# A hybrid decoder layer in float32: two more raw chunks in the up projection's ring, and four plain units at the head of the first down pair

## The chip, the cores and the metric

The kernel runs on one NeuronCore of a Trainium2 chip. The metric is the device time of one launch, in microseconds. Before the change the median of three runs was 1467.55 us (1465.33 to 1468.01). The engines are called TensorE (PE; its weight loads are PEld), VectorE (DVE), ScalarE (ACT), GpSimd (POOL) and SyncE (SP). SP and POOL issue the DMAs.

## The reference, cut to what matters

One layer of a decoder with 256 tokens and a width of 2048, in float32. The change touches the second half, the convolutional feed-forward part, and its weights `w_up` (2048 x 11264) and `w_down` (5632 x 2048):

```python
def conv_ffn(h, w_up, conv_w, conv_b, w_down):
    S = h.shape[1]
    a, b = jnp.split(h @ w_up, 2, axis=-1)
    ap = jnp.pad(a, ((0, 0), (CONV_WIDTH - 1, 0), (0, 0)))
    c = conv_b
    for j in range(CONV_WIDTH):
        c = c + conv_w[j] * ap[:, j:j + S]
    return (jax.nn.gelu(c, approximate=True) * b) @ w_down

def reference(x, ...):
    h = rms_norm(x, norm_mix_pre[l])
    y = hybrid_mixer(h, ...)              # latent attention, windowed attention, gates, output projection
    x = x + rms_norm(y, norm_mix_post[l])
    h = rms_norm(x, norm_ffn_pre[l])
    y = conv_ffn(h, ffn_w_up[l], ffn_conv_w[l], ffn_conv_b[l], ffn_w_down[l])
    return x + rms_norm(y, norm_ffn_post[l])
```

## The kernel before

**Arithmetic.** Every large product runs in a float32 format that TensorE takes at full rate, with each operand split into a high part and a low remainder. A product of two operands is three matmuls (high by high, high by low, low by high), which `mm3` issues. Weights come from HBM as a raw float32 chunk of 128 x 1024 (512 KB). `convert` (L135) then makes two tiles of it: ACT casts the raw chunk to `whi` (L144), and DVE subtracts that from the raw chunk to get `wlo` (L145). So each chunk needs one DMA, one ACT pass, one DVE pass, and then its matmuls.

**The rings.** Raw chunks lie in a ring of `RAW = 3` tiles, converted pairs in a ring of `RING = 4` pairs. Two more tiles, the `flex` tiles, serve either as two more raw chunks or as one more converted pair; `flex[0]` says which, and `in_turn` (L111) decides for each new chunk. `more_raw` is a list of makers of raw tiles through which `raw_row` (L151), the loader of single rows of weights, turns when it is not empty; `wchunk` (L117), the loader of the general chunks, doesn't look at it. A raw tile is free again once ACT and DVE have read it, a converted pair once PE has.

**Order of the work.** The program is traced in one order, with a clock of steps: each chunk of a product ends with `tick()`, and `at(t, f)` puts a piece of other work at step t. A planner then orders each engine's instructions by this trace order, by when their inputs should be there and by when a buffer is free; it can issue work earlier than it was traced where its buffer is free (the parked copies of the residual, traced in c = 2, run before the up projection). Each engine, and each DMA queue's issuer, works through its list in order: an instruction that waits holds up all behind it.

**The up projection.** `ffn_up0` makes the first 512 columns of both halves, then `ffn_up(c, ...)` (L1269) runs for c = 1 to 5 and, after the first part of the down projection, for c = 6 to 10. Each makes 512 columns of the activation half and 512 of the gate half with one call of `gemm_cols` (L1250) for each: eight chunks, and for each chunk eight matmuls of 512 columns (L1257, weight high by activations high and low) and eight of 256 (L1261, weight low by activations high). Tiles `ua` and `ub` are the two accumulators. `evac` brings them out (L1278 and L1279), and `conv_cols` (L1148) does the convolution, the GELU and the split of the result in four pieces, at the steps 1, 3, 5 and 7 of the chunks that follow.

**The down projection.** After c = 5, 24 of the 44 blocks of 128 inner columns are there. `pair_gemm` (L253) takes them in 12 units of two blocks, for 1024 output columns at a time; two such pairs, `d0` and `d1`, make the 2048 columns. A *plain* unit (letter p) converts two rows of weights and needs 8 products, 24 matmuls of 512 columns. A *seven* unit (letter s) uses a scheme of seven products, 21 matmuls; it needs sums of the tokens and sums of the weights, and 3.5 chunks of raw data: two of stored sums, one row and a half row of weights. `PAIR_ORDER` gives the order of the letters; the seven units take the first units in number, the plain ones the rest. At the start of the pairs the `flex` tiles turn to raw chunks, and eight steps later `deep_raws` (L1317) turns them back and puts seven raw tiles into `more_raw`: the ring and four tiles that held the evacuated accumulators.

**The sums.** `park_sums` (L221) makes the weight sums of a seven unit ahead of time: POOL loads two chunks into one tile of 128 x 2048 with the tag `gp` (L229), DVE makes four subtractions in it (L233), POOL stores the two halves to DRAM (L238, L243). Four units are done early; the others run during c = 1 to c = 4, one every 7 or 8 steps. `g_sums(u)` (L1242) makes the token sums of unit u, with `token_sums` (L347 to L353) and a split (L386, L387): six DVE instructions and one of ACT. Its results lie in tiles of two units each: units 0 and 1 in the tile of the first half of the tokens' residual (tag `x2_0`), 2 and 3 in that of the second half (`x2_1`), 4 and 5 in `gp`. Those two tiles are free because `park` (L1228) has stored the residual to DRAM; it is loaded again near the end.

After c = 10 the rest of the inner columns goes through another pair and two plain products.

Of the kernel before, what the change touches and what calls it, by code (L numbers as in the profile page):

```python
# [11 lines left out]
F32 = mybir.dt.float32  # L12
# [7 lines left out]
P = 128  # L20
D = 2048
# [21 lines left out]
def trunk_layer(ctx, tc, x, x_cols_in, conv_cols_in, g_mix_post, g_ffn_post, w_in, w_q, w_kv,  # L43
# [16 lines left out]
    def sb(pl, shape, name, dt=F32, tag=None, bufs=None):  # L60
        return pl.tile(shape, dt, name=name, tag=tag or name, **({"bufs": bufs} if bufs else {}))
# [46 lines left out]
    def ring_tile(kind, name, dt, extra):  # L108
        pl_tag = dict(name=name, tag="flex", bufs=2) if extra else dict(name=name, tag=kind, bufs=RAW if kind == "raw" else RING)
        return ring.tile([P, 1024], dt, **pl_tag)  # L110

    def in_turn(kind):

        turn[kind] += 1
        return flex[0] == kind and turn[kind] % (RAW + 2 if kind == "raw" else RING + 1) >= (RAW if kind == "raw" else RING)

    def wchunk(src, shape, own=None, rawp=None, rbufs=1, parts=None):  # L117
        i = cnt[0]
        cnt[0] += 1
        n = int(np.prod(shape))  # L120
        raw = rawp.tile([P, 1024], F32, name=f"raw{i}", tag="xraw", bufs=rbufs) if rawp else \
            ring_tile("raw", f"raw{i}", F32, in_turn("raw"))
        dst = raw[:, :n]
        if len(shape) == 2:
            dst = dst.rearrange("p (a b) -> p a b", a=shape[0])
        elif len(shape) == 3:
            dst = dst.rearrange("p (a b c) -> p a b c", a=shape[0], b=shape[1])
        if len(shape) == 3:
            for k in range(shape[0]):
                nc.sync.dma_start(dst[:, k], src[:, k])  # L130
        else:
            nc.sync.dma_start(dst, src)
        return convert(raw, n, own=own, parts=parts)
# [11 lines left out]
            vec.tensor_tensor(lo[:, a:b], raw[:, a:b], hi[:, a:b].bitcast(F32), op=ALU.subtract)  # L145
        return hi, lo

    more_raw = []
    raw_of = lambda name: ring_tile("raw", name, F32, False)

    def raw_row(src, n=1024):  # L151
        i = cnt[0]
        cnt[0] += 1
        if more_raw:
            make = more_raw.pop(0)
            more_raw.append(make)
            raw = make(f"raw{i}")
        else:
            raw = ring_tile("raw", f"raw{i}", F32, in_turn("raw"))
        nc.sync.dma_start(raw[:, :n], src)  # L160
        return raw

    steps = defaultdict(list)
    now = [0]

    def at(t, *fs):
        steps[max(t, now[0])].extend(fs)
# [53 lines left out]
    def park_sums(name, w, k, c0, pl, tag, t0, bufs=None):  # L221

        td = [dram.tile([P, 1024], F32, name=f"{name}{i}") for i in range(2)]
        st = []

        def load():
            st.append(sb(pl, [P, D], f"{name}s", tag=tag, bufs=bufs))
            for i in range(2):
                pool.dma_start(st[0][:, i * 1024:(i + 1) * 1024], w[(k + i) * P:(k + i + 1) * P, c0:c0 + 1024])  # L229

        def less(o, x, y):
            o, x, y = (st[0][:, i * 512:(i + 1) * 512] for i in (o, x, y))
            tc.keep_in_program_order(vec.tensor_tensor(o, x, y, op=ALU.subtract))  # L233

        def even():
            less(0, 1, 0)
            less(1, 3, 1)
            pool.dma_start(td[0], st[0][:, 0:1024])  # L238

        def odd():  # L240
            less(3, 3, 0)
            less(2, 2, 3)
            pool.dma_start(td[1], st[0][:, 1024:2048])  # L243

        at(t0 - 5, load)
        at(t0, even)
        at(t0 + 1, odd)
        return td

    def park_a(i, pl, tag, t0, **kw):  # L250
        return park_sums(f"ta{i}_", w_down, 2 * (i % NA), 1024 * (i // NA), pl, tag, t0, **kw)

    def pair_gemm(name, w, k0, c0, order, act_of, s_of, kind, d, place=None, sums=None, parked=None):  # L253

# [478 lines left out]
    acc, _ = gemm(XH, XL, w_in, 0, KT, 0, 512)  # L733
# [4 lines left out]
    acc, _ = gemm(XH, XL, w_in, 0, KT, C_KV, KVR + ROPE)  # L738
# [71 lines left out]
    parked_a = [park_a(i, pg, "gr", now[0] + 5 + 5 * i, bufs=2) for i in range(EARLY)]  # L810
# [158 lines left out]
    for j in range(4):  # L969
        acc, _ = gemm(XH, XL, w_in, 0, KT, C_GA + 512 * j, 512)  # L970
# [9 lines left out]
    es3, p3 = open_pool("p3")  # L980
# [49 lines left out]
    for j in range(4):  # L1030
# [4 lines left out]
        acc, _ = gemm(AH, AL, wo_a, 0, KT, 512 * j, 512, ps=(pss, "s") if j == 3 else None)  # L1035
# [190 lines left out]
    gtiles, s_pool, s_of = [], [], {}  # L1226

    def park(t, j):  # L1228
        pool.dma_start(x2_d[t, :, j * 512:(j + 1) * 512], x2[t][j])
# [4 lines left out]
        c = slice(j * 512, (j + 1) * 512)  # L1234
        nc.sync.dma_start(x2_all[t][:, c], x2_d[t, :, c])

    s_tiles = []

    def sums_tile(name, i):
        return sb(*((p3,) if i < 2 else (p6,)), [P, D], f"{name}_{i}", F32R, tag=(f"x2_{i}" if i < 2 else "gp"))  # L1240

    def g_sums(u):  # L1242

        if u % 2 == 0:
            s_tiles.append(sums_tile("s", u // 2))
        hi, lo = (s_tiles[u // 2][:, (u % 2) * 1024 + i * 512:(u % 2) * 1024 + (i + 1) * 512] for i in range(2))
        a, m = (sb(s_pool[0], [P, 512], f"s{n}{u}", tag="hx", bufs=2) for n in "am")
        s_of[u] = token_sums(gtiles[u].bitcast(F32), a, m, hi, lo)
# [40 lines left out]
            at(now[0] + 1 + 2 * i, lambda i=i: conv_cols(4 * c + i, sa[0][i], sa[1][i], slot0 + i))  # L1289

    es7 = ffn_up0()
    for i in range(2 * NA - EARLY):
        parked_a.append(park_a(i + EARLY, p6, "gp", now[0] + 8 + 15 * i // 2))
    for c in range(1, 6):
        if c == 2:
            for i in range(8):
                at(now[0] + i, lambda i=i: park(i // 4, i % 4))
        if c == 4:
            for u in range(4):
                at(now[0] + 3 + 3 * u, lambda u=u: g_sums(u))  # L1300
        if c == 5:
            for u in range(4, NA):
                at(now[0] + 3 + 5 * (u - 4), lambda u=u: g_sums(u))
        ffn_up(c, 4 * c)

    def down(k0, nk, c0, n, split=None, ps=None):
# [16 lines left out]
    for p in range(2):  # L1323
        d = [dsum[t][2 * p + j] for t in range(NT) for j in range(2)]
        c = pair_gemm(f"d{p}", w_down, 0, 1024 * p, PAIR_ORDER[p], lambda k, t: (GH(k)[:, t * P:(t + 1) * P], GL(k)[:, t * P:(t + 1) * P]),
                      lambda u: s_of[u], p, d, parked=parked_a[NA * p:NA * (p + 1)])
        for n_, (o, x_) in enumerate(zip(d, c)):
            at(now[0] + n_, lambda o=o, x_=x_: vec.tensor_tensor(o, o, x_, op=ALU.add))
    more_raw.clear()
# [11 lines left out]

    parked_b = [park_sums(f"tb{i}_", w_down, 24 + 2 * i, 0, p6, "gp", now[0] + 6 + 8 * i) for i in range(NB_)]
    for c in range(6, 11):
        if c == 9:
            for u in range(NB_):
                at(now[0] + 2 + 4 * u, lambda u=u: b_sums(u))
        ffn_up(c, 4 * (c - 6))
# [174 lines left out]
```

## Time and profile before

| | |
|---|---|
| median of three runs | 1467.55 us |
| runs, lowest and highest | 1465.33 and 1468.01 us |
| the profiled execution, its own time | 1472.41 us |
| its span, first to last instruction | 1470.6 us |
| granted TensorE clock over the span | 0.998 |
| up projection c = 1 to 5, with the end of `ffn_up0` | 776.1 to 1006.3 us |
| the two down pairs | 1006.3 to 1133.3 us |
| up projection c = 6 to 10 | 1133.3 to 1357.7 us |

The page counts an engine as busy from the start of an instruction to its modelled end. Matmuls are pipelined, and PE is shown as busy for almost the whole span; lost time is better seen in how long a fixed piece of work takes, for instance one call of `gemm_cols`, which is always the same 128 matmuls. The idle time of ACT and DVE costs nothing as long as PE finds its weights converted.

### The profile page before, as it was taken

How to read it: one execution, taken by the hardware profiler on the slowest of the kernel's cores; microseconds unless marked ns; L12 is line 12 of the kernel's file. 1: busy time of each engine (PE TensorE's matmuls, PEld its weight loads, DVE VectorE, ACT ScalarE, POOL GpSimd, SP SyncE). 2: the span in 40 equal slices, each digit the busy share in tenths (PEclk: the TensorE clock that was granted, in tenths of full speed). 3: DMA queues.
4: the chain of work that ended last, by engine and by line, in shares of the span. 5: the costliest groups of instructions: out<-in, count | busy, mean ns of one | idle time of the engine just before them, and what ended most of it. 6: DMA issues, size and time to landing. Idle time of an engine off the chain costs nothing.

```text
span 1470.6 us, 21276 instructions
## 1 busy us (share of the span) xinstructions
PE 1453.6 (99%) x7543; PEld 1239.7 (84%) x7543; DVE 1119.9 (76%) x1959; ACT 850.3 (58%) x1403; POOL 98.6 (7%) x176
## 2 busy tenths in 40 slices
PE   9999999999999999999999999999999999999997
PEld 7888888888888888888888888787888888888886
DVE  7788896766667666768799877677777778887776
ACT  7588874544565554446666554565655555566653
POOL 0012110010000011100000001000000000000000
PEclk9999999999999999999999999999999999999999
DMA  8755386697665559765767778777887888767973
GB/s 294 218 173 164 96 271 195 213 338 243 187 160 156 172 168 335 258 185 176 223 215 222 259 264 286 244 221 264 276 276 264 274 270 263 247 207 252 334 240 133
DMA packets 163302, 339.53 MB, mean 231 GB/s; under 512 B 20171, under 2 KB 31340, under 8 KB 163196
## 3 DMA queue, kind: packets, MB, share of 16 engines
q1 hardware_dynamic: 145888, 277.25, 59.4%
q0 software_dynamic: 17216, 60.88, 12.2%
q8 instruction: 59, 0.97, 0.3%
q14 instruction: 47, 0.39, 0.1%
q10 hardware_dynamic: 92, 0.05, 0.0%
HBM read 310.82 MB, written 27.31 MB: 230 GB/s over the span
## 4 chain that ended last, share of the span: by engine, by line
PE 75%; DVE 10%; DMA 9%; ACT 3%; issue 2%; DVEq 0%; ACTq 0%; SPq 0%
PE accg L184 12%; PE accg L186 12%; PE accg L185 12%; DMA raw<-in_ffn_w_up_dram 8%; PE ua L1257 4%; DVE wlo L145 4%; PE ub L1257 3%; PE ua L1261 2%; PE cd L185 2%; PE cd L186 2%; PE cd L184 2%; ACT whi L144 2%; PE ub L1261 2%; DVE ta_s L233 1%; PE mpo L948 1%
## 5 line engine op out<-in xcount | busy, mean ns | idle before, releaser
L145 DVE TENSOR_TENSOR wlo<-raw,whi 128x1024 fp32r<-128x1024 f32 (+2 forms) x526 | 624.5, 1195 | 243.0 <-ACT whi L144 238.0
L144 ACT CAST whi<-raw 128x1024 fp32r<-128x1024 f32 (+2 forms) x526 | 537.0, 1028 | 431.0 <-PE accg L186 157.3
L184 PE MATMUL accg<-whi,ahl 128*128 128x512 f32 (+1 forms) x416 | 162.8, 391 | 0.0
L186 PE MATMUL accg<-whi,ahl 128*128 128x512 f32 (+1 forms) x416 | 160.6, 386 | 0.0
L185 PE MATMUL accg<-wlo,ahl 128*128 128x512 f32 (+1 forms) x416 | 159.8, 384 | 0.0
L1257 PE MATMUL ub<-ahl,whi 128*128 128x512 f32 x640 | 154.6, 391 | 0.0
L1257 PE MATMUL ua<-ahl,whi 128*128 128x512 f32 x640 | 154.6, 391 | 0.0
L184 PE MATMUL accg<-whi,bhl 128*128 128x512 f32 x378 | 148.2, 392 | 0.0
L186 PE MATMUL accg<-whi,bhl 128*128 128x512 f32 x378 | 147.4, 390 | 0.0
L185 PE MATMUL accg<-wlo,bhl 128*128 128x512 f32 x378 | 147.3, 390 | 0.0
L1257 PEld LDWEIGHTS ua<-ahl,whi 128*128 128x128 f32 x640 | 117.6, 188 | 22.7
L1257 PEld LDWEIGHTS ub<-ahl,whi 128*128 128x128 f32 x640 | 117.5, 188 | 22.6
L186 PEld LDWEIGHTS accg<-whi,ahl 128*128 128x128 f32 x416 | 78.1, 188 | 15.5
L1261 PEld LDWEIGHTS ub<-ahl,wlo 128*128 128x128 f32 x640 | 82.5, 191 | 8.1 <-DVE wlo L145 4.8
L185 PEld LDWEIGHTS accg<-wlo,ahl 128*128 128x128 f32 x416 | 78.2, 188 | 13.1
L184 PEld LDWEIGHTS accg<-whi,ahl 128*128 128x128 f32 x416 | 78.2, 188 | 13.0
L1261 PE MATMUL ub<-ahl,wlo 128*128 128x256 f32 x640 | 84.5, 283 | 4.0 <-DVE wlo L145 4.0
L1261 PEld LDWEIGHTS ua<-ahl,wlo 128*128 128x128 f32 x640 | 82.4, 191 | 5.1 <-DVE wlo L145 1.9
L1261 PE MATMUL ua<-ahl,wlo 128*128 128x256 f32 x640 | 84.4, 283 | 1.5 <-DVE wlo L145 1.5
L186 PEld LDWEIGHTS accg<-whi,bhl 128*128 128x128 f32 x378 | 71.0, 188 | 14.8
L185 PEld LDWEIGHTS accg<-wlo,bhl 128*128 128x128 f32 x378 | 71.0, 188 | 14.4
L184 PEld LDWEIGHTS accg<-whi,bhl 128*128 128x128 f32 x378 | 71.0, 188 | 14.4
(573 smaller groups left out, 2336.8 us busy)
## 6 DMA issues: line engine op xcount, KB each, us to landing
raw<-in_ffn_w_up_dram SPq DMA_DIRECT2D x176, 512.0 KB, 4.7
raw<-in_w_in_dram SPq DMA_DIRECT2D x105, 512.0 KB, 4.6
raw<-in_ffn_w_down_dram SPq DMA_DIRECT2D x70, 512.0 KB, 5.2
raw<-in_w_o_swa_dram SPq DMA_DIRECT2D x32, 512.0 KB, 4.9
raw<-in_w_o_mla_dram SPq DMA_DIRECT2D x32, 512.0 KB, 5.0
raw<-in_w_out_dram SPq DMA_DIRECT2D x26, 512.0 KB, 4.2
ta_s<-in_ffn_w_down_dram POOLq DMA_DIRECT2D x24, 512.0 KB, 6.2
ta<-ta_s POOLq DMA_DIRECT2D x24, 512.0 KB, 5.2
```

The costliest lines, as they stand in the source:

```text
L144: act.copy(hi[:, a:b], raw[:, a:b])
L145: vec.tensor_tensor(lo[:, a:b], raw[:, a:b], hi[:, a:b].bitcast(F32), op=ALU.subtract)
L184: pe.matmul(o, ah, bh, start=start, stop=False)
L185: pe.matmul(o, ah, bl, start=False, stop=False)
L186: pe.matmul(o, al, bh, start=False, stop=stop)
L233: tc.keep_in_program_order(vec.tensor_tensor(o, x, y, op=ALU.subtract))
L948: pe.matmul(o, w(t), p_[:, c], start=n == 0, stop=n == 5)
L1257: pe.matmul(acc[i], hi[:, c], hn[p][:, j * 512:(j + 1) * 512], start=p + j == 0, stop=stop)
L1261: pe.matmul(acc[i][:, 0:256], lo[:, c], hn[p][:, j * 512:j * 512 + 256], start=False, stop=False)
```

## The change

There are two parts.

First, the choice of a raw tile moves into a function `new_raw`, which takes its tiles from `more_raw` when that list is not empty, and `wchunk` uses it as well as `raw_row`. A new function `x_raws` takes a tile with the tag `x2_1`, the one that held the second half of the residual, and fills `more_raw` so that the raw ring's three tiles alternate with the two halves of that tile: five raw chunks in place of three. It runs at step 8 of c = 2, and the list is emptied at step 6 of c = 5; it runs again at step 1 of c = 6 and is emptied at step 5 of c = 9. Since `x2_1` is taken in that time, the token sums of units 2 and 3 move: units 0 and 1 are traced in c = 4, and in c = 5 come units 4, 5, 2 and 3, at the steps 0, 4, 8 and 11.

Second, the order of the first down pair has four plain units at its head and five of seven products in all, in place of two and six. `NA` becomes a list with the number of seven units of each pair, so that eleven pairs of weight sums are stored in place of twelve.

```diff
+    more_raw = []
+    raw_of = lambda name: ring_tile("raw", name, F32, False)
+
+    def new_raw(name):
+        if not more_raw:
+            return ring_tile("raw", name, F32, in_turn("raw"))
+        more_raw.append(more_raw.pop(0))
+        return more_raw[-1](name)
+
     def wchunk(src, shape, own=None, rawp=None, rbufs=1, parts=None):
...
-            ring_tile("raw", f"raw{i}", F32, in_turn("raw"))
+            new_raw(f"raw{i}")
...
     def raw_row(src, n=1024):
         i = cnt[0]
         cnt[0] += 1
-        if more_raw:
-            make = more_raw.pop(0)
-            more_raw.append(make)
-            raw = make(f"raw{i}")
-        else:
-            raw = ring_tile("raw", f"raw{i}", F32, in_turn("raw"))
+        raw = new_raw(f"raw{i}")
...
     def park_a(i, pl, tag, t0, **kw):
-        return park_sums(f"ta{i}_", w_down, 2 * (i % NA), 1024 * (i // NA), pl, tag, t0, **kw)
+        u, p = (i, 0) if i < NA[0] else (i - NA[0], 1)
+        return park_sums(f"ta{i}_", w_down, 2 * u, 1024 * p, pl, tag, t0, **kw)
...
+    def x_raws():
+        t = sb(p3, [P, D], f"xraw{now[0]}", tag="x2_1")
+        more_raw[:] = [raw_of, lambda name: t[:, 0:1024], raw_of, lambda name: t[:, 1024:2048], raw_of]
...
-    for i in range(2 * NA - EARLY):
+    for i in range(sum(NA) - EARLY):
         parked_a.append(park_a(i + EARLY, p6, "gp", now[0] + 8 + 15 * i // 2))
     for c in range(1, 6):
         if c == 2:
             for i in range(8):
                 at(now[0] + i, lambda i=i: park(i // 4, i % 4))
+            at(now[0] + 8, x_raws)
         if c == 4:
-            for u in range(4):
+            for u in range(2):
                 at(now[0] + 3 + 3 * u, lambda u=u: g_sums(u))
         if c == 5:
-            for u in range(4, NA):
-                at(now[0] + 3 + 5 * (u - 4), lambda u=u: g_sums(u))
+            at(now[0] + 6, more_raw.clear)
+            for u, t in ((4, 0), (5, 4), (2, 8), (3, 11)):
+                at(now[0] + t, lambda u=u: g_sums(u))
         ffn_up(c, 4 * c)
...
-                      lambda u: s_of[u], p, d, parked=parked_a[NA * p:NA * (p + 1)])
+                      lambda u: s_of[u], p, d, parked=parked_a[NA[0] * p:])
...
     for c in range(6, 11):
+        if c == 6:
+            at(now[0] + 1, x_raws)
         if c == 9:
+            at(now[0] + 5, more_raw.clear)
             for u in range(NB_):
                 at(now[0] + 2 + 4 * u, lambda u=u: b_sums(u))
         ffn_up(c, 4 * (c - 6))
...
-PAIR_ORDER = ("ppspspsspssp", "ppspspsspssp")
+PAIR_ORDER = ("ppppspsspssp", "ppspspsspssp")
 EARLY = 4
-NA = PAIR_ORDER[0].count("s")
+NA = [o.count("s") for o in PAIR_ORDER]
```

More of the change, by code (lines that the diff above doesn't have):

```diff
@@ L146, in convert @@
         return hi, lo
-    more_raw = []
-    raw_of = lambda name: ring_tile("raw", name, F32, False)
     def raw_row(src, n=1024):
@@ L1235, in unpark @@
         nc.sync.dma_start(x2_all[t][:, c], x2_d[t, :, c])
-    s_tiles = []
+    s_tiles = {}
     def sums_tile(name, i):
         return sb(*((p3,) if i < 2 else (p6,)), [P, D], f"{name}_{i}", F32R, tag=(f"x2_{i}" if i < 2 else "gp"))
+    def x_raws():
+        t = sb(p3, [P, D], f"xraw{now[0]}", tag="x2_1")
+        more_raw[:] = [raw_of, lambda name: t[:, 0:1024], raw_of, lambda name: t[:, 1024:2048], raw_of]
     def g_sums(u):
         if u % 2 == 0:
-            s_tiles.append(sums_tile("s", u // 2))
+            s_tiles[u // 2] = sums_tile("s", u // 2)
         hi, lo = (s_tiles[u // 2][:, (u % 2) * 1024 + i * 512:(u % 2) * 1024 + (i + 1) * 512] for i in range(2))
```

## The prediction

> **What bounds the kernel now.** I read the page first (engines, chain), then the busy time by stretch over the feed-forward part, then the chain of waits and the waits inside the stretches that stood out.
>
> ```profile
> span 1470.6 us, 21276 instructions
> ...
> PE 1453.6 (99%) x7543; PEld 1239.7 (84%) x7543; DVE 1119.9 (76%) x1959; ACT 850.3 (58%) x1403; POOL 98.6 (7%) x176
> ```
>
> TensorE is the bound, so time can only go where it waits, or through fewer matmuls. I cut the feed-forward part at the first matmul of each call of `gemm_cols` and of the down pairs (rows: stretch, its length, busy time and instructions of PE, PEld, DVE, ACT and POOL, granted clock, DMA share, GB/s):
>
> ```profile
> 867.20:889.40 22.20, 22.20 (x129) 19.66 (x128) 17.42 (x31) 10.31 (x17) 2.13 (x4) 1.00 0.74 238
> 889.40:984.10 94.70, 90.32 (x514) 79.03 (x513) 71.40 (x119) 50.33 (x82) 6.40 (x12) 1.00 0.78 257
> 984.10:1006.30 22.20, 22.20 (x129) 19.65 (x128) 17.03 (x27) 13.11 (x22) 0.00 (x0) 1.00 0.74 225
> 1006.30:1034.00 27.70, 25.56 (x104) 19.94 (x103) 18.50 (x27) 15.58 (x24) 0.00 (x0) 0.94 0.76 266
> 1034.00:1133.30 99.30, 99.30 (x440) 82.23 (x439) 73.64 (x74) 58.94 (x62) 1.06 (x2) 1.00 0.84 279
> ...
> 1222.40:1268.70 46.30, 45.24 (x258) 39.61 (x257) 38.05 (x67) 25.42 (x42) 4.26 (x8) 1.00 0.81 263
> 1268.70:1357.70 89.00, 89.00 (x513) 78.67 (x513) 69.27 (x115) 54.04 (x88) 1.07 (x2) 1.00 0.73 231
> ```
>
> An undisturbed call takes 89.00 / 4 = 22.25 us (last row), that is 2.78 us for each of its 8 chunks of 512 KB. Three places lose time. 889.4 to 984.1 holds four calls (second half of c = 3 to the first half of c = 5): 94.7 - 89.0 = **5.7 us lost**. 1222.4 to 1268.7 holds two (c = 8): 46.3 - 44.5 = **1.8 us**. The two down pairs have 2 x (6 x 24 + 6 x 21) = 540 matmuls; 438 of them fill the 99.3 us from 1034.0 (the row counts two more, cut by its edges), 0.227 us each; the other 102 should take 23.1 us and took 27.7: **4.6 us** at the head of the first pair. Together 12.1 us; everywhere else here PE runs without a break, and that is the ceiling of any gain.
>
> What the up projection waits for, in the chain of waits (start, duration, what) and in the waits of 889 to 984 (total, times, longest):
>
> ```profile
> 938.04 1.06 ACT whi L144
> 939.12 1.24 DVE wlo L145
> 940.37 9.95 DMA raw<-in_ffn_w_up_dram
> 950.41 1.05 ACT whi L144
> ```
> ```profile
> ACT whi L144 <- DMA raw<-in_ffn_w_up_dram: 28.4, 14, 6.2
> ```
> ```profile
> SPq L132 <- DVE wlo L145: 28.6, 15, 3.2
> ```
> ```profile
> raw<-in_ffn_w_up_dram SPq DMA_DIRECT2D x65, 512.0 KB, 4.8
> ta_s<-in_ffn_w_down_dram POOLq DMA_DIRECT2D x14, 512.0 KB, 6.6
> ```
>
> The first rows are one turn of the raw ring: DVE finishes a chunk, only then does SP issue the load that takes its slot, and ACT starts when that lands. A slot is held for load + cast + subtraction: 4.8 (median of the third fence) + 1.05 + 1.24 = 7.1 us, with the 9.95 us load 12.2 us. Three slots come round every 3 x 2.78 = 8.3 us. The median just fits, any load over 6.0 us doesn't, and the lead in converted weights is eaten until PE stops. Loads get that long while POOL loads a parked pair beside them:
>
> ```profile
> 939.80 1.06 POOL L229 DMA_DIRECT2D ta_s<-in_ffn_w_down_dram  x2 [5.96 <-DMA ta<-ta_s]
> ```
>
> **The change, part by part.**
>
> *Five raw slots instead of three, c = 2 to c = 5 and c = 6 to c = 9.* Five slots come round every 13.9 us, more than the longest slot time above (12.2 us). So the waits of both up stretches should go. Not all of it: at 5.7 + 1.8 us I keep 1.3, because DVE also stands before the parked rows, and because the engines are fuller in the stretch that loses first:
>
> ```profile
> 889.40:912.70 23.30, 22.67 (x129) 19.79 (x129) 17.90 (x31) 11.91 (x21) 2.58 (x5) 1.00 0.90 315
> ...
> 961.20:984.10 22.90, 22.59 (x131) 19.76 (x129) 18.69 (x33) 13.81 (x23) 0.00 (x0) 1.00 0.68 198
> ```
>
> The bounds are 0 saved (that 0.90 is a ceiling) and 7.5; without the waits the stretch needs 257 x 94.7 / 89.0 = 273 GB/s, below the 315 that were moved, so I stand near the upper end: **-6.2 us**.
>
> *Where the two slots come from.* The second residual tile has to be parked before. Its stores were issued at 739.4 and took 5.7 us in the median, 100 us before the tile is wanted (c = 2, step 8, two calls before 889), so SP never stands at its first load:
>
> ```profile
> 739.40 2.53 POOL L1229 DMA_DIRECT2D x_d<-x  x4 [3.28 <-DVE x L1068]
> ```
> ```profile
> x_d<-x POOLq DMA_DIRECT2D x8, 256.0 KB, 5.7
> ```
>
> In the second half the tile is free when units 2 and 3 of the second pair are done, the eighth of its twelve units, some 20 us before c = 6. Cost 0; without that cover SP, with all loads behind it, would wait for the rest of it.
>
> *The token sums.* The sums of units 2 and 3 lived in that tile and were made early (the first sum of all ran at 807.7). Now they must wait for the last chunk in it, and run in the second half of c = 5 beside those of 4 and 5.
>
> ```profile
> L347 DVE TENSOR_TENSOR sa<-bhl x6: 682/683/693, 807.7 to 891.2; 128x512 f32<-128x512 f32 x6
> ```
> ```profile
> L350 DVE TENSOR_TENSOR sm<-sa x6: 282/283/293, 820.4 to 964.7; 128x128 f32<-128x128 f32 x6
> ...
> L387 DVE TENSOR_TENSOR s<-sm,s x6: 680/684/691, 829.8 to 967.7; 128x512 fp32r<-128x512 f32 x6
> ```
>
> One set is 0.68 + 4 x 0.28 + 0.68 = 2.5 us of DVE, so 5.0 us move into c = 5, whose two calls have 18.69 + 17.03 = 35.7 us in the rows above. 40.7 of 44.5 us still fits, with the slots back to three but no parked traffic (198 and 225 GB/s). The cover is a lead of some four converted chunks; if it is gone, the whole 5.0 us shows. I take 0.
>
> *One unit plain instead of seven products in the first pair.* 24 matmuls instead of 21, all on PE: 3 x 0.227 = **+0.7 us**. On the other side 3.5 chunks become 2, and one parked pair (two loads, four subtractions, two stores) is gone from c = 4; it is the very pair at 939.8 that stood beside the 9.95 us load.
>
> *Four plain units at the head.* Chain of waits around the old head:
>
> ```profile
> 1002.81 7.20 DMA raw<-in_ffn_w_down_dram
> ...
> 1010.11 1.06 ACT whi L144
> 1011.19 1.24 DVE wlo L145
> ...
> 1012.47 0.50 PE cd L185
> ...
> 1020.10 1.05 ACT whi L144
> 1021.17 1.24 DVE wlo L145
> ...
> 1023.76 0.43 PE qd L186
> ```
> ```profile
> 1021.19 0.50 PE L184 MATMUL qd<-whi,s 128*128 128x512 f32 x1 [1.10 <-ACT whi L144]
> 1022.45 0.50 PE L185 MATMUL qd<-wlo,s 128*128 128x512 f32 x1 [0.76 <-DVE wlo L145]
> ```
> ```profile
> 1002.81 1.05 ACT L144 CAST whi<-raw 128x1024 fp32r<-128x1024 f32 x1 [1.44 <-PE ub L1257]
> 1010.11 1.05 ACT L144 CAST whi<-raw 128x1024 fp32r<-128x1024 f32 x1 [6.25 <-DMA raw<-in_ffn_w_down_dram]
> ```
> ```profile
> 1020.00:1034.00 14.00, 12.14 (x46) 9.55 (x46) 9.97 (x10) 8.92 (x11) 0.00 (x0) 0.88 0.70 235
> ```
>
> The flex slots change sides here, so the third and fourth row wait until PE gives up a weight pair (load at 1002.81, landed 1010.0); ACT stands meanwhile, and the evacuation and convolution of c = 5 pile up behind its cast. PE waits 0.4 us at 1012.47. Then the first unit of seven asks for 3.5 chunks in 21 x 0.227 = 4.8 us, the pile is still there, PE stops twice (1.1 and 0.8 us), and then the granted clock falls (0.88 over 14 us: 1.7 us lost; matmuls at 0.43 instead of 0.23 us). In the new order the same two slots change sides, so the 0.4 us stays. But rows five to eight are plain: one cast and one subtraction for 12 matmuls, 2.7 us. The first seven comes 4 x 24 x 0.227 = 21.8 us after the start instead of 10.9, with step 8 reached, hence on the seven deep slots of `deep_raws`; from there the order is letter for letter what the old one has from its own step 8, and that ran without a break (1034.0 on). I keep 0.9 of the 4.6 us: the 0.4 and as much again. Bounds 0 and 4.6; I take **-3.7 us**, because the stretch from 1034.0 is the same work.
>
> *The new `new_raw`*, moved code and dictionaries: names only, 0.
>
> Sum: -6.2 + 0.7 - 3.7 = **-9.2 us** on the profiled execution (1472.41 us: the span and 1.8 around it), which stands 4.9 us above the median. Where those 4.9 lie no view shows; if all lay in the 12.1 us of waits, the plain runs could gain only 4.3, if none, 9.2. I take 1 us off for it: 1467.55 - 8.2 = **1459.3 us**.
>
> **The rivals.**
>
> *A. The DMA engines are the limit, not the slots.* More loads in flight then only take longer each, and PE goes on waiting where POOL loads. For it: the 9.95 us load under two POOL loads, and 0.90 in the first stretch that loses. Against it: 0.78 over the whole stretch. Of the 7.5 us only the wait that followed the removed pair would go (24.80 us for a call, 2.5 lost):
>
> ```profile
> 936.40:961.20 24.80, 22.55 (x129) 19.75 (x129) 16.46 (x27) 11.90 (x20) 2.14 (x4) 1.00 0.75 258
> ```
>
> Gain 2.5 + 3.7 - 0.7 = 5.5, less 1: about 1463.0 us. The Trainium skill, DMA: Bandwidth & Descriptors, section "Issuing engines are not separate DMA queues", speaks for this one: loads from all issuing engines run on the same 16 engines and interleave. The trace agrees that they interleave (9.95 us against a median of 4.8); whether depth helps all the same, no run here shows yet.
>
> *B. The head of the pair stalls again, elsewhere.* The third row still lands late, ACT still stands 6 us, the pile of c = 5 is the same; if PE outruns the casts once more, the stop and the slow clock come back. Against it: 2.7 us of PE for each 1.2 us of DVE. Gain 6.2 - 0.7 = 5.5, less 1: 1463.0 us. By the Trainium skill, TensorE: Matmul & The Clock Gate, Part 1, half clock follows an idle window of some 3.4 us; here two stops of 1.1 and 0.8 us were enough, so by the page a short stop would cost B nothing more, and by this trace it can.
>
> *C. Slower: the two halves of the residual's tile are not tracked apart.* Then a load into one half waits until the chunk in the other is converted: two such waits in each round of five slots, at least 2 x (4.8 + 1.05 + 1.24) = 14.2 us against 13.9, and 2 x 8.9 = 17.8 with the 6.6 us that loads take beside POOL. Over the 98 chunks that use the ring, some 20 rounds, 6 to 78 us; in the middle 42, less the 3.0 of the head: about 1506 us. It decides as soon as a load passes 4.7 us. Against it: the row at 939.80, two loads into the two halves of one tile issued within 1.06 us, the second without waiting for the first.
>
> *D. No change.* c = 5 has 5.0 us more DVE work, loses its slots at step 7, and hands the down pair empty weight rings. Three chunks of lead lost at 2.8 us each take back 8.3 us: 1467.6 us. For it: DVE at 40.7 of 44.5 us. Against it: at the old end of c = 5 (the row at 1002.81) ACT was waiting for PE to free a weight pair, so the lead was whole.
>
> **How the numbers follow.** My case 0.62; A 0.10; B 0.13; C 0.08; D 0.07. What a measurement can tell from no change is 0.2%, 2.9 us; my case, A and B all gain more: faster 0.85, same 0.07 (D), slower 0.08 (C). Range: if all waits go, 12.1 - 0.7 = 11.4 us, 1456.1, and 1 us for the spread of the runs: 1455. Above, A and B at 1463.0, and 2.5 us more if A keeps the removed pair's wait too: 1465.5. C and D lie outside, 0.15.
>
> **What would show it.** In the profile after, each call of `gemm_cols` from c = 3 to c = 8 should take 22.2 to 22.5 us; casts waiting for loads may stay, PE waiting for `wlo` must not. SP should issue w_up loads four or five chunks ahead. The head of the first pair should show one short wait at the third row and no stretch of half clock; four sets of sums in c = 5. Calls still over 23 us with loads over 8 us: A. SP issues of `raw` that wait for the subtraction two chunks back: C. A stop at 1020 to 1030: B or D. I would be wrong above all if five slots do not cover the loads under POOL's traffic.

## The result, and the profile after

The changed kernel takes 1461.71 us (median of six runs, 1461.18 to 1462.22) where the kernel before took 1467.07 us in the same session (six runs, 1465.33 to 1470.95). The ratio is 0.9961, with a 95% interval of 0.9948 to 0.9974. The forecast was 1459.3 us with a range of 1455.0 to 1465.5. So the time lies in the range, 2.4 us above the forecast, and the gain is 5.4 us where 8.2 were forecast. The kernel before spreads widely, and in a later set of runs beside it the changed kernel gained 6.6 us.

The page of the profile of the changed kernel, the busy times and the shares of the chain that ended last:

```profile
PE 1449.6 (99%) x7546; PEld 1238.6 (85%) x7546; DVE 1117.3 (77%) x1953; ACT 850.2 (58%) x1401; POOL 96.4 (7%) x172
...
PE 94%; DVE 3%; ACT 2%; issue 1%; DMA 1%; DVEq 0%; ACTq 0%
```

There are three matmuls more, as counted. Before, the same line of the chain read:

```profile
PE 75%; DVE 10%; DMA 9%; ACT 3%; issue 2%; DVEq 0%; ACTq 0%; SPq 0%
```

So what left the chain is DMA and, behind it, DVE and ACT: the turns of the raw ring. The busy time by stretch shows where (columns as in the prediction; the cuts are again the first matmuls of the calls and of the pairs):

```profile
845.60:890.20 44.60, 44.60 (x258) 39.38 (x257) 38.37 (x65) 24.62 (x41) 4.85 (x10) 1.00 0.89 306
890.20:979.30 89.10, 89.10 (x514) 78.77 (x513) 71.99 (x123) 52.89 (x86) 4.23 (x8) 1.00 0.72 230
979.30:1001.50 22.20, 22.20 (x129) 19.64 (x128) 14.91 (x26) 11.28 (x21) 0.00 (x0) 1.00 0.79 261
1001.50:1024.60 23.10, 23.10 (x103) 19.14 (x102) 15.25 (x24) 12.58 (x19) 0.00 (x0) 1.00 0.57 201
...
1213.60:1258.20 44.60, 44.60 (x258) 39.40 (x257) 37.07 (x63) 25.27 (x41) 3.21 (x6) 1.00 0.78 263
```

The four calls that took 94.7 us take 89.1, the two of c = 8 take 44.6 instead of 46.3, and the first 102 matmuls of the first pair take 23.1 instead of 27.7, at full clock. In each of these rows PE is busy for the whole stretch: of the 12.1 us of waits nothing is left. (Between the calls of c = 1 there is one wait of 0.26 us that before didn't have, at 806.7 us; two of the experiments show a like one, the others none; it was not followed up.)

Why PE no longer waits is best seen at ACT, which makes the first half of each converted pair. What ACT waited for in 890 to 1000 us (total, times, longest), first in the kernel before, then in the changed one:

```profile
ACT whi L144 <- DMA raw<-in_ffn_w_up_dram: 31.1, 16, 6.2
```
```profile
ACT whi L153 <- PE ub L1263: 11.0, 6, 4.5
ACT whi L153 <- PE ua L1263: 7.7, 6, 2.7
ACT whi L153 <- PE ua L1267: 1.7, 2, 0.9
ACT whi L153 <- PE ub L1267: 0.9, 1, 0.9
```

Before, the casts of ACT stood 31.1 us because raw data was late. After, they stand 21.3 us, and always because PE has not yet given up a converted pair: in this profile the conversion is as far ahead as its ring lets it be. The loads themselves did not get faster (issues in 800 to 1001 us of the changed kernel, the last number is the median from issue to landing; before it was 4.8):

```profile
raw<-in_ffn_w_up_dram SPq DMA_DIRECT2D x48, 512.0 KB, 5.0
xraw<-in_ffn_w_up_dram SPq DMA_DIRECT2D x16, 512.0 KB, 5.6
```

### The profile page after: what moved, and what is told of

The parts are those of the page before. It is cut to its first block, busy times and chain, and to the rows that moved or that the text cites. A ratio compares the mean times of both kernels' runs of the same rounds, so it can differ in the third digit from the quotient of the medians.

```text
span 1460.2 us, 21246 instructions
## 1 busy us (share of the span) xinstructions
PE 1449.6 (99%) x7546; PEld 1238.6 (85%) x7546; DVE 1117.3 (77%) x1953; ACT 850.2 (58%) x1401; POOL 96.4 (7%) x172
## 3 DMA queue, kind: packets, MB, share of 16 engines
q0 software_dynamic: 16640, 58.78, 11.8%
## 4 chain that ended last, share of the span: by engine, by line
PE 94%; DVE 3%; ACT 2%; issue 1%; DMA 1%; DVEq 0%; ACTq 0%
PE accg L185 11%; PE accg L187 11%; PE accg L186 11%; PE ub L1263 10%; PE ua L1263 10%; PE ub L1267 5%; PE ua L1267 5%; PE cd L187 2%; PE cd L186 2%; PE cd L185 2%; PE mpo L950 1%; PE cdb L187 1%; PE cdb L185 1%; PE cdb L186 1%; PE cg L185 1%; PE cg L187 1%
## 5 line engine op out<-in xcount | busy, mean ns | idle before, releaser
L154 DVE TENSOR_TENSOR wlo<-raw,whi 128x1024 fp32r<-128x1024 f32 (+2 forms) x485 | 575.3, 1194 | 214.7 <-ACT whi L153 207.3
L153 ACT CAST whi<-raw 128x1024 fp32r<-128x1024 f32 (+2 forms) x485 | 495.0, 1027 | 384.2 <-PE accg L187 155.0
```

Source lines behind the costliest of these rows:

```text
L153: act.copy(hi[:, a:b], raw[:, a:b])
```

## The experiments

Two theories stood against each other over the head of the pair. *Own cause*: the old head stalls by its own order (the flex tiles change sides, sevens come early), as the prediction had it; then the ring alone leaves the 4.6 us there. *Inherited*: the up projection arrives at the pair with hardly any converted chunks in hand, and the head stalls for that; then the ring alone heals it. How many it has in hand is called the *lead* below: the time from the end of DVE's subtraction of a chunk to the first matmul that reads its result. A third, rival A, says that the DMA engines are the limit. The expectations were written as the study went on, so the lead appears in them in earlier forms than the one it ends with. Times are compared within a set of runs on the same chip; every ratio is to the kernel before in that set.

**The kernel before, profiled twice more.** No edit. The question is whether the 12.1 us are a property of the kernel.

> The kernel before once more, unchanged, for a second profile. The first profile's own time stood 4.9 us above the median and held 12.1 us of waits in the feed-forward part. If taking a profile makes the loads late, this profile holds 11 to 13 us of waits again and its span is again near 1470 us. If the waits only differ from execution to execution, it can lie anywhere between 1462 and 1472 us, with its waits smaller by as much as its span is.

> The kernel before, a third profile. As for the second: waits of 11 to 13 us in the feed-forward part if the profiling makes them, anything from 2 to 13 if they differ from execution to execution.

Measured: 1467.64 and 1464.81 us. What PE's weight loads waited for in the feed-forward part up to c = 10 (776 to 1360 us) in the three profiles of the same kernel, the one of the prediction first:

```profile
PEld ub L1261 <- DVE wlo L145: 4.8, 4, 2.5
PEld ua L1261 <- DVE wlo L145: 1.9, 2, 1.4
PEld qd L184 <- ACT whi L144: 1.5, 1, 1.5
PEld qd L185 <- DVE wlo L145: 1.1, 1, 1.1
PEld cd L185 <- DVE wlo L145: 0.9, 2, 0.7
```
```profile
PEld ub L1261 <- DVE wlo L145: 2.4, 4, 1.0
PEld ua L1261 <- DVE wlo L145: 2.4, 3, 1.2
PEld qd L184 <- ACT whi L144: 1.4, 1, 1.4
PEld qd L185 <- DVE wlo L145: 1.1, 1, 1.1
```
```profile
PEld ub L1261 <- DVE wlo L145: 2.3, 3, 1.5
PEld qd L185 <- DVE wlo L145: 1.1, 1, 1.1
PEld qd L184 <- ACT whi L144: 0.8, 1, 0.8
PEld ua L1261 <- DVE wlo L145: 0.6, 1, 0.6
```

The sums are 10.2, 7.3 and 4.8 us. The first profile has 1.7 us of half clock on top. Taken off the times of these three executions they leave 1472.41 - 11.9 = 1460.5, 1467.64 - 7.3 = 1460.3 and 1464.81 - 4.8 = 1460.0 us: the same kernel, with a different amount of waiting in each execution. It is not the profiler's doing: the runs of this kernel in all sets, 71 of them, lie between 1461.41 and 1473.63 us, median 1468.7, and the three profiled executions lie among them.

**The ring alone.** Five slots, but the old order of the pair with six sevens and all twelve parked pairs of sums; the diff is against the changed kernel.

```diff
-PAIR_ORDER = ("ppppspsspssp", "ppspspsspssp")
+PAIR_ORDER = ("ppspspsspssp", "ppspspsspssp")
```

> The ring of five raw slots in both stretches, with the old order of the first down pair (six of seven products, two plain units at the head, twelve parked pairs). My theory, each part removes the waits of its own stretch: the calls of the up projection all take 22.3 us, although the eighth parked pair in the up projection is back; the head of the first pair waits some 4.6 us as before; profile 7.5 us under the first profile of before, 1463 us of span. Plain runs hold about half of the waits that the profile held (6.5 of 12.1), so 4 us under before, about 1463. Rival A, the DMA engines are the limit and the removed pair did it: a call at c = 4 still takes over 24 us and the time is within 1.5 us of before.

Measured: 1460.15 us (six runs, 1459.90 to 1460.88), ratio 0.9944 (0.9925 to 0.9964). Its profile has no wait of PE for a converted weight anywhere between 776 and 1360 us, the old head included. Its stretches of the second half of c = 3 to the first half of c = 5, and of the head:

```profile
890.20:979.30 89.10, 89.10 (x514) 78.78 (x513) 73.78 (x127) 50.48 (x83) 6.40 (x12) 1.00 0.78 256
...
1001.50:1024.60 23.10, 23.10 (x104) 19.14 (x103) 17.94 (x27) 14.70 (x21) 0.00 (x0) 1.00 0.69 233
```

The first row has the same twelve POOL loads and stores (x12) and the same 256 GB/s as the row that lost 5.7 us before (257 GB/s at a share of 0.78). The traffic is the same and the waits are gone, so the slots were the limit and not the DMA engines: rival A falls. The second row has the old order, and no wait: *own cause* falls too. What changed at the head shows in SP's issues. Before (the pair starts at 1006.37):

```profile
1002.81 1.70 SPq L160 DMA_DIRECT2D raw<-in_ffn_w_down_dram  x3
```

and with the ring alone (the pair starts at 1001.19):

```profile
992.37 1.69 SPq L161 DMA_DIRECT2D raw<-in_ffn_w_down_dram  x3
```

The same group of three rows is issued 3.6 us ahead of the pair in the one and 8.8 us ahead in the other. The order of SP's list is the same there in both profiles; only the time is different.

**The new order alone.** Three slots throughout, four plain units at the head, five sevens; the diff is against the changed kernel.

```diff
-            at(now[0] + 8, x_raws)
...
-        if c == 6:
-            at(now[0] + 1, x_raws)
```

(The token sums of units 0 to 3 then stay where they were.)

> The new order of the first down pair alone (four plain units at its head, five of seven products, eleven parked pairs), with three raw slots and the old places of the token sums. My theory: the calls from c = 3 to the start of c = 4 still lose 2 to 3 us in the profile, the one at the removed pair loses nothing, c = 8 still loses 1.8; the head of the pair waits 0.4 us at the third row and has no stretch of half clock. Profile 4.6 + 2.5 - 0.7 = 6 us under before; plain runs 2.5 + 1.4 - 0.7 = 3 us under, about 1464. Rival: the head only runs clean because the ring of five hands it a longer lead; then it stops here too, by 2 us or more, and the time is that of before.

Measured: 1465.29 us (twelve runs, 1463.07 to 1469.80), ratio 0.998 (0.9965 to 0.9994). In its profile the head and the first stretch run without a wait; c = 7 and 8 wait:

```profile
PEld ub L1267 <- DVE wlo L154: 3.5, 4, 1.5
PEld ua L1267 <- DVE wlo L154: 2.3, 1, 2.3
```

So the order has some worth where the slots are few, 0.2%; but it and the ring do not add up. This profile does not test the head itself: the last chunk of c = 5 has a lead of 6.8 us there, near the 7.6 us at which the old order loses nothing either (see the end of this section). That the first stretch ran clean was not expected, nor were 5.8 us of waits in c = 7 and 8.

**Six sevens, three plain at the head**, otherwise the changed kernel.

```diff
-PAIR_ORDER = ("ppppspsspssp", "ppspspsspssp")
+PAIR_ORDER = ("pppsspsspssp", "ppspspsspssp")
```

> The changed kernel with three plain units at the head and still six of seven products (order pppsspsspssp), twelve parked pairs. 21 matmuls in place of 24 in one unit: 0.7 us less for PE. If the lead that the plain units build carries the two units of seven that follow, 0.7 us under the changed kernel, about 1461.0. If the fourth plain unit is needed at the head, PE stops there by 2 us or more, perhaps with half clock behind it, and it is 1.5 to 3 us slower than the changed kernel, 1463 to 1465.

Measured: 1461.10 us (eight runs, 1460.38 to 1462.07), ratio 0.9951 (0.9934 to 0.9968). One wait appears, at the second of the two sevens that now stand together:

```profile
PEld qd L186 <- DVE wlo L154: 0.7, 1, 0.7
```

Between the starts of its matmuls PE loses 0.4 us there, which gives back part of the 0.7 us that three matmuls fewer bring. Two sevens side by side are a little too fast for the conversion, though the lead at the end of c = 5 is 7.0 us here.

**The ring in the first stretch only.**

```diff
-        if c == 6:
-            at(now[0] + 1, x_raws)
```

> The changed kernel with the ring of five in c = 2 to c = 5 only; c = 6 to 10 have three slots as before. My theory: c = 8 loses its 1.8 us again in the profile, about 1 us in plain runs: 1462.7 against 1461.7 for the changed kernel. Rival: the second stretch lost time only because the first part of the kernel ran late; then nothing changes, 1461.7.

**Four slots instead of five**, one half of the tile left unused.

```diff
-        more_raw[:] = [raw_of, lambda name: t[:, 0:1024], raw_of, lambda name: t[:, 1024:2048], raw_of]
+        more_raw[:] = [raw_of, raw_of, raw_of, lambda name: t[:, 0:1024]]
```

> The changed kernel with one more raw slot in place of two (four slots: three of the ring and one half of the residual's tile). Four slots come round every 11.1 us, which is over the 7.1 us of a median load with its conversion and under the 12.2 us of the longest. My theory, depth against late loads: nearly all of the gain, with at most 0.5 us of waits left, 1461.7 to 1462.2. If the fifth slot is what carries it, half of the up projection's waits come back: 1463 or more.

Measured, side by side: 1463.54 us for the first stretch only (nine runs, 1462.50 to 1466.31; ratio 0.9967, 0.9953 to 0.9981), 1461.02 us with four slots (six runs, 1460.70 to 1461.90; ratio 0.9947, 0.9931 to 0.9963). The second stretch is worth some 2.5 us in plain runs (as far as four slots and five are equal in the first stretch), more than the 1.8 us that the first profile showed there. The profile of the first variant has all its waits for converted weights in c = 7 and 8; none are left in the first stretch and at the head:

```profile
PEld ub L1267 <- DVE wlo L154: 2.1, 4, 1.1
PEld ua L1267 <- DVE wlo L154: 1.0, 2, 0.7
```

So the second stretch does not stall because the first part ran late. And four slots are enough; the profile with four has no wait for a converted weight, and this is its stretch from c = 3 to c = 5:

```profile
890.20:979.30 89.10, 89.10 (x514) 78.76 (x513) 72.30 (x125) 52.86 (x87) 4.27 (x8) 1.00 0.74 239
```

Four slots come round every 4 x 2.78 = 11.1 us: more than the slot time of 7.1 us worked out from the median load, less than the 12.2 us of the longest. The longest load that its own profile has between 800 and 1001 us took 9.5 us, which makes a slot time of 11.8 us. So the ring need not cover the longest load: a single late one is carried by the converted pairs.

**The changed kernel and the ring alone once more**, together in one set.

> The changed kernel again, on the same chip as the next three. No waits of PE in the feed-forward part; runs within 1.5 us of each other, about 1461.5.

> The ring of five with the old order again, beside the changed kernel. Its profile had no wait at the head of the first pair, so the new order adds three matmuls and takes nothing away: 0.7 us under the changed kernel at least, 1.5 us as the two sessions read. If the difference of the sessions was that of the chips, the two are within 0.3 us.

Measured: 1461.49 us (six runs, 1460.15 to 1462.74; ratio 0.9954, 0.9940 to 0.9968) and 1460.27 us (six runs, 1459.00 to 1461.25; ratio 0.9946, 0.9932 to 0.9960). Neither profile has a wait left. The old order is the faster one by 1.2 us; its three matmuls fewer account for 0.7 us, and the rest lies within the spread of the runs. The ring alone has the matmuls of the kernel before and none of its waits, and its two sets, 1459.00 to 1461.25 us, lie where the three executions above lie once their waits are taken off. In the first set it was also ahead of the version with six sevens and three plain units at the head (1460.15 against 1461.10), which has as many matmuls and the wait of 0.4 us. The ring with the old order is the best version found, and beats both kernels.

**Where the lead is made.** With the ring, is the lead at the head made up to the last moment, or is it made in c = 2 and 3 and kept? Here the five slots end at the start of c = 4, so that its parked pairs meet three slots again. Old order; the second stretch keeps its ring; the diff is against the ring alone.

```diff
         if c == 4:
+            more_raw.clear()
             for u in range(2):
...
-            at(now[0] + 6, more_raw.clear)
```

> The ring of five with the old order, but back to three slots at the start of c = 4 in place of step 6 of c = 5. New theory: the head of the first pair waits because the lead was lost before it, under the parked pairs of c = 4 (the third row's load is issued 3.6 to 4.8 us ahead of the pair in the three profiles of before, 8.8 in the ring of five). Then here that load is issued some 5 us ahead again and the head loses 1.5 to 4.5 us: 1462 to 1464 in plain runs. My first theory (the burst of the units of seven at the head) has no say on it. If the order of the loads that the planner makes is what differs, the head stays clean: 1460.2.

Measured: 1460.57 us (six runs, 1459.91 to 1461.48), ratio 0.9949 (0.9936 to 0.9963): as good as the full ring. My version of the theory, that the lead is lost under the parked pairs of c = 4, fell. Here is what ACT waited for in 890 to 1000 us:

```profile
ACT whi L153 <- DMA raw<-in_ffn_w_up_dram: 13.6, 9, 3.3
ACT whi L153 <- PE ub L1263: 7.7, 4, 4.5
ACT whi L153 <- PE ua L1263: 5.3, 5, 1.6
```

It is between the two kernels: data is late nine times, and still the conversion comes back to waiting for PE. A lead once gained in c = 2 and 3 lasts over c = 4 and 5 on three slots. In this profile it is never under 5.8 us there. The kernel before loses its lead earlier: its first profile has 4.8 to 12.8 us of lead in c = 1, and 0.1 us at the last chunk of c = 3 (the leads are worked out by matching DVE's subtractions with PE's chunks in their order).

**Two plain units at the head and five sevens**, three slots: the new order's smaller number of parked pairs without its head. The diff is against the kernel before; the list `NA` and `park_a` are as in the changed kernel.

```diff
-PAIR_ORDER = ("ppspspsspssp", "ppspspsspssp")
+PAIR_ORDER = ("ppspspsspspp", "ppspspsspssp")
```

> Three slots everywhere, five units of seven in the first pair, but only two plain units at its head (order ppspspsspspp), eleven parked pairs. It tells the two halves of the new order apart. Lead theory: the removed parked pair at the end of c = 4 is what helps, the third row's load is issued some 8 us ahead and the head is clean or loses under 1 us; time as for the new order alone, 1465.3. My prediction's reading: the two plain units more at the head are what helps, so without them PE stops at the first unit of seven, with 2 to 4.6 us lost: 1467 to 1469.

Measured: 1467.51 us (twelve runs, 1461.99 to 1472.40), ratio 0.9998 (0.9982 to 1.0014). Its spread is that of the kernel before, and its profile has small waits in the first stretch (1.4 us over two calls) and at the head (0.8 us). A parked pair fewer brings nothing that can be measured. Against the 0.998 of the order with four plain units the difference is 0.2%, and the intervals overlap: that four plain units at the head help a kernel with three slots is likely from this pair and not settled.

**The ring in the second stretch only**, old order; the diff is against the ring alone.

```diff
-            at(now[0] + 8, x_raws)
```

(Again the sums of units 0 to 3 stay where they were.)

> The ring of five in c = 6 to c = 9 only, three slots in the first half, old order, twelve parked pairs. No waits at c = 7 and 8; c = 3 to c = 5 and the head of the first pair wait as in the kernel before, differing from execution to execution: 2 to 10 us in a profile, 1463 to 1469 in plain runs with a median 1.5 to 3 us under before. The head should have no waits where the third row's load is issued over 8 us ahead of the pair, and wait where it is issued under 5.

Measured: 1467.24 us (eleven runs, 1464.58 to 1469.30), ratio 0.9985 (0.9975 to 0.9994). In its profile c = 8 is clean and the first stretch and the head wait. The four calls cut at even places, the stretch behind the stop at the head, and c = 8:

```profile
890.00:979.00 89.00, 85.66 (x491) 75.23 (x490) 67.67 (x114) 49.45 (x81) 6.39 (x12) 1.00 0.79 257
...
1018.00:1032.00 14.00, 12.72 (x48) 10.15 (x49) 10.22 (x9) 8.96 (x11) 0.00 (x0) 0.88 0.69 229
1213.00:1258.00 45.00, 45.00 (x260) 39.76 (x259) 37.90 (x65) 24.84 (x40) 4.26 (x8) 1.00 0.85 283
```

This is the picture of the kernel before with its last part healed: 2.2 to 2.8 us (from the ratio, and from the medians of its set), in agreement with the 2.5 us above.

Put side by side, the lead of the last chunk of c = 5 and what PE then lost at the head, in the profiles with two plain units at the head: 2.5 us of lead and 4.7 lost, the half clock counted in (before), 3.2 and 4.0, half clock again (ring in the second stretch only), 3.3 and 2.3, 3.7 and 1.7 (before, the two repeats), 4.8 and 0.8 (two plain, five sevens), then 7.6 and 7.7 (ring alone, twice) and 7.8 (ring up to c = 4) and nothing. The loss falls as the lead grows, without an exception. The load of the third row moves with the lead: in all of these profiles it is issued 1.1 us further ahead of the pair than the lead is long (3.6 us with 2.5 before, 4.8 with 3.7 in the second repeat, 8.8 with 7.7 in the ring alone).

## Why the prediction was right, and where it was off

**Five slots let the waits of the up projection go: right, and for the reason given.** The calls in the rows above take 22.2 to 22.3 us each, the waits of ACT's casts have turned from loads to PE, and the ring alone shows it at unchanged traffic. The term of -6.2 us was too small for the profile it was made against: the 1.3 us that were kept for full engines and parked rows did not stay, all 7.5 went. The ceiling feared there, 0.90 of the DMA engines' time, was reached and was none: the two calls from 845.6 us ran at 0.89 and 306 GB/s without a wait of PE. The 273 GB/s that the stretch from c = 3 to c = 5 was to need were too many: with the ring alone it moved 256.

**Four plain units at the head, -3.7 us: the mechanism was wrong.** The wait and the half clock did go, but the ring alone removes them with the old order in place. The step read the chain backwards from the stop and ended at what stood next to it, the flex tiles and the sevens. That the third row was issued only 3.6 us before the pair was seen and put down to the flex tiles changing sides, with SP waiting until PE gives up a weight pair. That reading was wrong. What SP stood for between 990 us and the start of the pair, in the kernel before (of its waits before the loads for the pair, the largest and the one for PE; the others, 2.9 us, are for DVE too):

```profile
SPq L160 <- DVE uu L1159: 5.5, 2, 3.4
SPq L160 <- PE ub L1261: 0.5, 1, 0.5
```

SP's list kept pace with DVE, which was late with the last chunks of c = 5; it was the up projection's lost lead that held the row back. So this part gains nothing beside the ring, and its price, +0.7 us for three matmuls, is right by count and 1.2 us by the runs. The 0.4 us at the third row, which "stays", and as much again, did not stay either.

**The token sums in c = 5, 0 us: right in size, not in the reason.** They cost nothing, but the cover was hardly tried, because most of their work did not move. The first sum of each of the six sets, in the changed kernel:

```profile
L349 DVE TENSOR_TENSOR sa<-bhl x6: 683/688/693, 808.4 to 936.7; 128x512 f32<-128x512 f32 x6
```

The last one starts at 936.7 us, and c = 5 begins at 957.0: the planner made the sums earlier than they were traced. Only four small sums and two splits, 2.5 us, run in the first call of c = 5, as much as before the change, so the 5.0 us more that were to come there did not come. DVE has 16.5 and 14.9 us of work in the two calls, 31.4 where the prediction had 40.7. **The tile's two halves, 0 us: right in size, not in the reason.** The cover that was counted on, 100 us between the parking of the residual and the tile's first use, was not there: the planner put the first two loads into the halves far ahead of where they are traced. SP's list stood for the residual's stores before them, in 735 to 800 us of the changed kernel:

```profile
SPq L141 <- DMA x_d<-x: 9.5, 2, 8.9
```

All eight profiles that take the tile in c = 2 have such a stand, 7.2 to 9.0 us at the longest, the others none. It cost PE nothing: no matmul waits in the changed kernel from 745 to 800 us.

**From the profiled execution to the median: the step that was off.** The prediction took 1 us off for the 4.9 us by which that execution stood above the median, because no view showed where they lay. The two repeats show it: in the waits, all of them. An execution of this kernel is 1460.0 to 1460.5 us plus whatever it waits, and the change takes the waits away whichever they are. So the waits of one profile may be taken only from the time of that execution: 1472.41 - 12.1 + 0.7 = 1461.0 us. In the forecast's own terms: 1459.3, plus the other 3.9 of those 4.9 us, less the 1.3 and 0.9 that were kept and went, is 1461.0; measured 1461.71. The two errors were of opposite sign, and that they partly cancel is luck. So is the place of half the gain: the 3.7 us of the new order were in the sum for a wrong reason, and the time came out near because the ring removed those waits too. The remaining 0.7 us stays open; profiled executions with the same matmuls and no wait in this part differ by nearly as much among themselves (1460.57 us in the second one of the ring alone, 1461.18 with the ring up to c = 4).

**The rivals.** A fell with the ring alone, as told. The Trainium skill, DMA: Bandwidth & Descriptors, section "Issuing engines are not separate DMA queues", says that loads from all issuing engines share and interleave on the same 16 engines. The runs agree in that the loads got no faster (5.0 and 5.6 us in the median against 4.8). They show that depth pays all the same, because a longer load that was issued earlier still lands in time. B did not come: no stop at the head. C did not come: SP issued the first loads into the two halves at 749.51 and 749.93 us, the second long before the first had landed (3.9 us after its issue). D would have shown as waits at the head for lack of lead; the lead of the last chunk was 9.2 us, and there were none.

## What to carry to other kernels

When a kernel's waits come from late loads, its time differs from execution to execution, and the time without waits is the number to predict: take the waits of a profile from the time of that same execution, not from the median. A stall at the head of a stage may be inherited: look at how far ahead the producers were in the stage before (does the converter wait for data or for a free buffer?) prior to redesigning the head. Where a second ring of converted data lies behind it, as here, a prefetch ring has to cover the usual time for which a slot is held, with some margin, not the longest; and of a change with two parts each should be run alone, since here the second part only cost time.

## What was not expected of the hardware

**Half clock comes and goes behind like stops.** Behind stops of PE at the head of the pair, the matmuls of the kernel with the ring in the second stretch only:

```profile
1018.52 0.50 PE L185 MATMUL qd<-whi,s 128*128 128x512 f32 x1 [1.00 <-ACT whi L153]
1019.78 0.73 PE L186 MATMUL qd<-wlo,s 128*128 128x512 f32 x1 [0.76 <-DVE wlo L154]
1020.30 0.63 PE L187 MATMUL qd<-whi,s 128*128 128x512 f32 x1
1020.73 0.63 PE L185 MATMUL qd<-whi,s 128*128 128x512 f32 x1
```

and of the first repeat of the kernel before:

```profile
1016.90 0.50 PE L184 MATMUL qd<-whi,s 128*128 128x512 f32 x1 [0.94 <-ACT whi L144]
1018.17 0.50 PE L185 MATMUL qd<-wlo,s 128*128 128x512 f32 x1 [0.76 <-DVE wlo L145]
1018.50 0.40 PE L186 MATMUL qd<-whi,s 128*128 128x512 f32 x1
1018.74 0.40 PE L184 MATMUL qd<-whi,s 128*128 128x512 f32 x1
```

The stops differ by 0.06 us; the matmuls then start 0.43 us apart in the one and 0.23 in the other. In both profiles with half clock (that of the ring in the second stretch only and the first of the kernel before) it lasted 3.4 us, and PE was busy for 1.64 and 1.54 us of the 3.4 us ahead of it. That is not enough for a rule: around the stops of the first repeat PE was busy for 1.71 us of 3.4 and kept its clock, and in the new order alone it was busy for 1.28 us around a single stop of 2.3 us at 1230.03, which was followed by ten microseconds at a granted clock of 1.00. The Trainium skill, TensorE: Matmul & The Clock Gate, Part 1, ties half clock to an idle window of some 3.4 us. None of these stops is that long, alone or in pairs, and still two profiles show it. What decides was not found.

**DVE stands for a parked pair once the ring gets deeper.** In the changed kernel SP issues five loads of the up projection within 846 to 855 us. The store of a parked pair that POOL issued at 846.52 takes 7.0 us beside them (5.2 us before), so the loads of the next parked pair are issued only at 854.04. DVE's first subtraction for that pair, at 859.03, stands 4.24 us for them, with the subtractions of the next chunks behind that in its list. All eight profiles with four or five slots in the first stretch have such a stand between 840 and 872 us, 3.0 to 5.9 us long, and none of the six with three slots has one. That SP's burst is the cause is likely and not shown: the kernel before issues five such loads within 843 to 854 us as well. From one chunk to the next the lead falls from 9.4 to 2.4 us, in the first profile of the ring alone to 0.7 us, and recovers. It cost nothing in these runs; a kernel that arrives with less lead might pay.
